# A hybrid decoder trunk on one core: another order of the first loads, and of the first gate weight ahead of the conformer

## The chip, the cores and the metric

The kernel runs on one core of a Trainium2 chip. The core has TensorE (PE), VectorE (DVE), ScalarE (ACT), GpSimd (POOL) and SyncE (SP), each with its own instruction stream, and 16 DMA engines that are fed from queues on SP, ACT and POOL. The metric is the time of one execution on the device, in microseconds (us), as the median of several runs.

## The reference, cut to what matters

Two layers work on 512 tokens of width 1024, all in float32. Layer 0 begins with a mixer, layer 1 with a conformer module; every layer goes on with cross-attention into 256 memory tokens and a gated MLP, each behind an RMSNorm and added to the residual.

```python
def rms_norm(x, g):
    y = xf * lax.rsqrt(jnp.mean(xf * xf, axis=-1, keepdims=True) + EPS)
    return (y * g).astype(x.dtype)

def conformer_conv(x, norm, w1, b1, dw_w, dw_b, ln_g, ln_b, w2, b2):
    h = rms_norm(x, norm) @ w1 + b1
    h = jax.nn.glu(h, axis=-1)
    h = causal_dwconv(h, dw_w, dw_b)
    h = jax.nn.silu(layer_norm(h, ln_g, ln_b))
    return h @ w2 + b2

def cross_attn(x, mem, norm, mem_norm, wq, wk, wv, wo):
    m = rms_norm(mem, mem_norm)
    k = (m @ wk).reshape(Bn, M, XA_HEADS, XA_HD)
    v = (m @ wv).reshape(Bn, M, XA_HEADS, XA_HD)
    ...
```

## The kernel before, in words

Activations lie feature by token: eight chunks X[0] to X[7] of 128 features by 512 tokens. Every matrix product is made of three: each operand is split into a high half (a copy rounded to the matmul's float type, on ACT: L170, L180, L204, L284) and a low half (the difference, on DVE: L171, L185, L207), and `mm3` (L190 to L192) adds high by high, high by low and low by high. So a weight of 128x1024 passes through DMA (tile `raw`, three buffers), ACT (`whi`) and DVE (`wlo`) before PE can use all of it, and its `raw` buffer comes free for a later load when DVE is done.

**Opening** (L1819 to L1924). The first work is the values of the cross-attention's memory, m @ wv: `mem.sums` (L458 to L469) takes one half of a weight a step, six products of 512 columns, L468. The gains `par` and the first half of the first weight are loaded from ACT's queue (L122, L123), all else from SP's in the written order: the memory's first half in pieces of 128x256 (L1836), the rest of the first weight, and so on, with the fourth weight behind the release of the first one's buffer. `mem.operand` splits a piece of the memory (ACT L399, DVE L400); `half` splits half a weight. Before that PE runs ten matmuls of 128x128 on a constant (L143), whose result nobody reads. In this stretch the order on PE, ACT, DVE, POOL and SP is the written one.

**Start of the conformer** (L1633 to L1673). The last weights of the MLP before it end in eight sums into X[n] (L911), each of which `Scaled.feed` (L254 to L259) follows with a square (ACT, L256) and an addition of the squares (DVE, L258). `norm.scale` then makes the factor of each token: column sums on PE (L324), a root (ACT, L331), a reciprocal (DVE, L332), two diagonal matrices (DVE, L337) and two products that spread them over the partitions (PE, L360). With it `norm.scaled`, `norm.high`, `norm.low` make each chunk of the normed input. As work for PE meanwhile there are keys of the second layer's memory (`mem.products` of parked weights: three pieces of 24 products of 256 columns), and then the first gate and value weights G0 and V0 multiply the normed chunks. Here Tile's scheduler sets the order of ACT and DVE by priority, except in the block of `norm.scaled/high/low`, which is written out, and from L1663 on, where all is written out again. `tc.issue_after(ins)` keeps an instruction behind `ins` on its engine.

Of the kernel before, what the change touches and what calls it, by code (L numbers as in the profile page):

```python
# [10 lines left out]
F32 = mybir.dt.float32  # L11
# [51 lines left out]
def trunk(ctx: ExitStack, tc: tile.TileContext, I: dict, out: list):  # L63
# [16 lines left out]
    def nm(s):  # L80
        uid[0] += 1
        return f"{s}_{uid[0]}"
# [7 lines left out]
    def big_f():  # L90
        return big.tile([P, 2 * T], F32, tag="big", name=nm("big"))
# [25 lines left out]
    G.memset(eps, EPS)  # L117
    A.activation(small.tile([P, 1], F32, tag="warm", name="warm", bufs=1), eps, AF.Copy)
    par = cpool.tile([P, NPAR], F32, tag="par", name="par")
    first_raw = wp.tile([P, D], F32, tag="raw", name="raw0", bufs=3)  # L120
    with tc.high_priority(AHEAD):
        A.dma_start(par[:, : 3 * C], I["params"][:, : 3 * C])  # L122
        A.dma_start(first_raw[:, :T], I["wv"][0][:, :T])  # L123
    xall = xpool.tile([P, C, T], F32, tag="x", name="x")
    X = [xall[:, c] for c in range(C)]

# [12 lines left out]
    V.tensor_copy(ones, onesf)  # L139

    idle = stat_ps()
    for _ in range(10):
        PE.matmul(idle[:, :P], onesf, onesf, start=True, stop=True)  # L143
    ident = cpool.tile([P, P], F32, tag="ident", name="ident")
    make_identity(nc, ident)
# [21 lines left out]
    def split(src, hi=None, lo=None, eng=None):  # L167
        hi = act_r() if hi is None else hi
        lo = act_r() if lo is None else lo
        A.activation(hi, src, AF.Copy)  # L170
        fetched[1] = (eng or V).tensor_tensor(lo, src, hi.bitcast(F32), op=ALU.subtract)  # L171
        return hi, lo
# [15 lines left out]
    def mm3(ps, w, x, first, last, onto=False):  # L188
        (wh, wl), (xh, xl) = w, x
        PE.matmul(ps, wh, xh, start=first, stop=False, skip_group_check=onto)  # L190
        PE.matmul(ps, wh, xl, start=False, stop=False, skip_group_check=onto)  # L191
        return PE.matmul(ps, wl, xh, start=False, stop=last, skip_group_check=onto)  # L192

    class Piece:


        def __init__(self, src, raw=None):
            self.raw = raw or wp.tile([P, D], F32, tag="raw", name=nm("raw"), bufs=3)
            fetched[0] = nc.sync.dma_start(self.raw, src)
# [9 lines left out]
    def blk(w, i, n=P):  # L209
        hi, lo = (w.hi, w.lo) if isinstance(w, Piece) else w  # L210
        if isinstance(hi, list):
            hi, lo, i = hi[i // T], lo[i // T], i % T
        return hi[:, i : i + n], lo[:, i : i + n]
# [33 lines left out]
    class Scaled:  # L247
# [6 lines left out]
        def feed(self, c):  # L254
            sq = tmp_f()
            self.square = A.activation(sq, X[c], AF.Square).ins  # L256
            if self.ss is not None:
                V.tensor_tensor(sq, self.ss, sq, op=ALU.add)  # L258
            self.ss = sq  # L259

        def scale(self):
# [65 lines left out]
    def token_scale(s, weight, halves):  # L327

        ps = token_sums(s, weight)
        rt = small.tile([P, 4], F32, tag="rtok", name=nm("rtok"), bufs=2)  # L330
        A.activation(rt, ps[:, :4], AF.Sqrt, bias=eps)  # L331
        V.reciprocal(rt, rt)  # L332
        return diagonals(rt, 4, halves)

    def diagonal(out, v, scale):
        n = v.shape[-1]
        V.scalar_tensor_tensor(  # L337
            out.rearrange("p (a b) -> p a b", a=n), ident.unsqueeze(1).broadcast_to([P, n, P]), scale,
            v.unsqueeze(2).broadcast_to([P, n, P]), op0=ALU.mult, op1=ALU.mult,
        )  # L340

    def diagonals(rt, n=4, halves=True):

# [37 lines left out]
    class Memory:  # L381
# [1 line left out]

        r = rt = None

        def __init__(self, layer, eng=None, load=True):
            self.layer, self.eng = layer, eng
            self.m = [big_f(), big_f()]
            self.xs = [None, None]
            if load:  # L390
                for h in range(2):
                    nc.sync.dma_start(self.m[h], I["mem"][h])
# [54 lines left out]
        def products(self, w, ps=None, ks=range(C)):  # L447
            ps = ps or mm_ps()
            for k in ks:
                mm3(ps[:, :M], blk(w, k * P), self.chunk(k), k == 0, k == C - 1)  # L450
            return ps

        def piece(self, i, **how):
# [1070 lines left out]
    def conformer(norm, nxt, mem, parked):  # L1524
# [88 lines left out]
        def warm(name, func, ins):  # L1613
            with tc.issue_after(ins):
                A.activation(small.tile([P, 1], F32, tag="warm", name=name, bufs=1), eps, func)
# [6 lines left out]
        def fetch():  # L1622
            if len(raws) < len(names):
                k, n = names[len(raws)][0], int(names[len(raws)][1:])
                src = I["pw1"][n + (C if k == "G" else 0)] if k in "GV" else I["wk" if k == "K" else "wv"][mem.layer * C + n]
                raws.append(wp.tile([P, D], F32, tag="raw", name=nm("raw"), bufs=3))
                Memory.fetched = nc.sync.dma_start(raws[-1], src)
# [2 lines left out]
            k = names[len(ws)]  # L1630
            ws[k] = load_w(raw=raws[len(ws)], eng=eng, park=k in ("R0", "R1", "R2", "R3"))

        for _ in range(2):  # L1633
            fetch()
            weights()
        for _ in range(3):
            fetch()
        warm("token", AF.Sqrt, norm.square)
        for n in range(KE):
            with tc.issue_after(mem.behind):  # L1640
                if n:
                    held = mem.products(parked[n])
                else:
                    mem.keys(n, parked[n])
            if n == 1:
                with tc.high_priority(URGENT):
                    norm.scale()
        with tc.high_priority(URGENT), tc.manual_schedule(engines={mybir.EngineType.Activation, mybir.EngineType.DVE}):
            norm.scaled(0)
            for c in range(C):  # L1650
                norm.high(c)
                if c + 1 < C:
                    norm.scaled(c + 1)
                norm.low(c)
                if c == 2:
                    split(held[:, :M], *mem.key(1))
            weights()
            fetch()
            weights()
# [157 lines left out]


    n0 = Scaled(("ab_norm", 0), False)  # L1819
    mem = Memory(0, load=False)  # L1820
    m = mem.m
    with tc.manual_schedule(engines=ORDERED | {mybir.EngineType.SP}):
        raws, ready = [first_raw], []

        def fetch(n, at=slice(0, D)):
            if n == len(raws):
# [3 lines left out]
        def half(n, i):  # L1830
            if n == len(ready):
                ready.append(tuple(wp.tile([P, D], F32R, tag=t, name=nm(t)) for t in ("whi", "wlo")))
            split(*[x[:, i * T : (i + 1) * T] for x in (raws[n], *ready[n])])

        for i in range(2):
            nc.sync.dma_start(m[0][:, i * M : (i + 1) * M], I["mem"][0][:, i * M : (i + 1) * M])  # L1836
        fetch(0, slice(T, D))
        nc.sync.dma_start(m[0][:, T:], I["mem"][0][:, T:])
        for i in range(2):
# [2 lines left out]
        fetch(2)  # L1842
        ps = [[mm_ps(), mm_ps()] for _ in range(2)]
        steps = mem.sums(0, ps[0], ready)
        for k in range(C):
            mem.operand(k // 4, [k % 4])
            half(k // 2, k % 2)
            next(steps)
            if k in (1, 3, 5, 7):
                fetch(k // 2 + 3)  # L1850
            if k == 3:
                nc.sync.dma_start(X[0], I["x"][0])
            elif k == 5:
                for c in (1, 2):
                    nc.sync.dma_start(X[c], I["x"][c])
# [155 lines left out]
```

## Time and profile before

| | us |
|---|---|
| median of 3 runs | 1419.03 (1418.37 to 1419.62) |
| the profiled execution | 1418.12 |
| its span in the trace | 1416.3 |
| PE busy in it | 1406.8 (99%) |
| DVE, ACT, POOL busy | 1142.8, 939.2, 317.8 |

The span is the time from the first to the last event that the profiler records; 1.8 us of the execution lie outside it. A timeline row gives the start, the duration, the engine, the line, the operation, output and input, and in brackets how long the engine had stood idle and what ended that.

### The profile page before, as it was taken

To read this page: it belongs to the slowest core of one execution; us is meant where nothing else is said; L and a number is where in the kernel's file an instruction comes from. 1 tells how busy PE (TensorE), PEld (TensorE's weight loads), DVE (VectorE), ACT (ScalarE), POOL (GpSimd) and SP (SyncE) were. 2 spreads that over 40 slices of the span, in tenths; PEclk is the share of its full clock that TensorE was granted. 3 is DMA by queue.
4 is the path that set the end of the run, shared out by engine and by line. 5 is a ranking of instruction groups with operands and counts; after the bars stand their busy time and mean duration, and the time that the engine had idled before them with its cause. 6 is when DMAs were issued, how large, how long until landed. Compare 5 with 4: busy or idle time off the path is not lost.

```text
span 1416.3 us, 21233 instructions
## 1 busy us (share of the span) xinstructions
PE 1406.8 (99%) x7700; PEld 1212.1 (86%) x7700; DVE 1142.8 (81%) x1932; ACT 939.2 (66%) x1692; POOL 317.8 (22%) x333
## 2 busy tenths in 40 slices
PE   9999999999999999999999999999999999999998
PEld 8888888998898888888888777899889888888887
DVE  6987776778877888888799997978788788788785
ACT  7678744776567676676666547766756766666664
POOL 0011310110122222222008993011002222212211
PEclk9999999999999999999999999999999999999999
DMA  8623232444387777677443454345438776776751
GB/s 309 194 75 103 91 119 82 111 121 128 99 204 173 164 180 178 162 180 170 122 119 119 120 157 156 105 90 131 111 101 194 174 179 164 174 182 163 169 136 60
DMA packets 80025, 204.22 MB, mean 144 GB/s; under 512 B 9008, under 2 KB 9520, under 8 KB 79920
## 3 DMA queue, kind: packets, MB, share of 16 engines
q1 hardware_dynamic: 50688, 149.89, 33.2%
q0 software_dynamic: 28800, 52.44, 21.6%
q8 instruction: 60, 0.98, 0.3%
q10 hardware_dynamic: 432, 0.54, 0.2%
q14 instruction: 45, 0.37, 0.1%
HBM read 145.16 MB, written 2.10 MB: 104 GB/s over the span
## 4 chain that ended last, share of the span: by engine, by line
PE 94%; DVE 3%; ACT 1%; DMA 1%; issue 1%; POOL 0%; ACTq 0%; POOLq 0%; DVEq 0%
PE mm L819 17%; PE mm L190 15%; PE mm L191 15%; PE mm L192 15%; PE aux L190 7%; PE aux L191 7%; PE aux L192 7%; PE stat L819 7%; PE mm L468 2%; PE mm L1569 1%; DVE wlo L171 1%; DVE act L171 1%; PE aux L542 0%; ACT whi L170 0%; PE aux L468 0%
## 5 line engine op out<-in xcount | busy, mean ns | idle before, releaser
L191 PE MATMUL mm<-act,whi 128*128 128x512 f32 (+2 forms) x779 | 288.1, 370 | 0.1
L190 PE MATMUL mm<-act,whi 128*128 128x512 f32 (+2 forms) x779 | 288.1, 371 | 0.0
L192 PE MATMUL mm<-act,wlo 128*128 128x512 f32 (+2 forms) x779 | 287.9, 370 | 0.0
L867 DVE TENSOR_TENSOR bigr<-raw,bigr 128x512 fp32r<-128x512 f32 x176 | 120.3, 686 | 62.7 <-ACT bigr L860 62.3
L190 PEld LDWEIGHTS mm<-act,whi 128*128 128x128 f32 x779 | 146.5, 188 | 25.7 <-ACT tmp L1594 0.8
L191 PEld LDWEIGHTS mm<-act,whi 128*128 128x128 f32 x779 | 146.8, 188 | 25.1 <-DVE act L171 1.0
L192 PEld LDWEIGHTS mm<-act,wlo 128*128 128x128 f32 x779 | 146.8, 188 | 24.7 <-DVE wlo L171 0.6
L860 ACT ACTIVATE bigr<-raw 128x512 fp32r<-128x512 f32 x176 | 109.3, 622 | 84.0 <-DVE wlo L207 81.5
L819 PE MATMUL mm<-bigr,bigr 128*128 128x512 f32 (+1 forms) x816 | 160.2, 338 | 0.0
L190 PE MATMUL aux<-act,whi 128*128 128x512 f32 x399 | 155.4, 390 | 0.0
L191 PE MATMUL aux<-act,whi 128*128 128x512 f32 x399 | 155.3, 389 | 0.0
L192 PE MATMUL aux<-act,wlo 128*128 128x512 f32 x399 | 155.2, 389 | 0.0
L873 POOL DMA_DIRECT2D raw<-wa x100 | 95.2, 972 | 254.0 <-DVE bigr L867 166.1
L170 ACT ACTIVATE whi<-raw 128x1024 fp32r<-128x1024 f32 (+1 forms) x95 | 96.2, 1019 | 83.9 <-PE mm L191 44.1
L819 PEld LDWEIGHTS mm<-bigr,bigr 128*128 128x128 f32 x816 | 120.9, 190 | 12.2
L870 POOL DMA_DIRECT2D raw<-raw x50 | 43.3, 866 | 385.6 <-DVE wlo L867 282.8
L171 DVE TENSOR_TENSOR wlo<-raw,whi 128x1024 fp32r<-128x1024 f32 (+1 forms) x75 | 90.3, 1210 | 19.9 <-ACT whi L170 19.6
L875 POOL DMA_DIRECT2D raw<-wa x50 | 43.1, 863 | 202.6 <-DVE bigr L867 91.1
L192 PEld LDWEIGHTS aux<-act,wlo 128*128 128x128 f32 x399 | 74.9, 188 | 15.8
L191 PEld LDWEIGHTS aux<-act,whi 128*128 128x128 f32 x399 | 74.9, 188 | 15.5
L190 PEld LDWEIGHTS aux<-act,whi 128*128 128x128 f32 x399 | 74.9, 188 | 15.4
L175 DVE TENSOR_TENSOR tmp<-mm,tmp 128x256 f32<-128x256 f32 x198 | 79.4, 418 | 3.4 <-PE mm L192 1.0
(384 smaller groups left out, 3336.1 us busy)
## 6 DMA issues: line engine op xcount, KB each, us to landing
raw<-wa POOLq DMA_DIRECT2D x150, 256.0 KB, 3.9
wa<-in_wpair SPq DMA_DIRECT2D x88, 256.0 KB, 3.7
raw<-in_wpair SPq DMA_DIRECT2D x44, 512.0 KB, 4.1
big<-in_wdown SPq DMA_DIRECT2D x42, 512.0 KB, 4.6
raw<-raw POOLq DMA_DIRECT2D x50, 256.0 KB, 4.0
raw<-in_pw SPq DMA_DIRECT2D x24, 512.0 KB, 3.9
raw<-in_win SPq DMA_DIRECT2D x20, 512.0 KB, 3.5
raw<-in_wk SPq DMA_DIRECT2D x16, 512.0 KB, 3.5
```

The source lines that it names most:

```text
L170: A.activation(hi, src, AF.Copy)
L171: fetched[1] = (eng or V).tensor_tensor(lo, src, hi.bitcast(F32), op=ALU.subtract)
L175: V.tensor_tensor(out, a, b, op=ALU.add)
L190: PE.matmul(ps, wh, xh, start=first, stop=False, skip_group_check=onto)
L191: PE.matmul(ps, wh, xl, start=False, stop=False, skip_group_check=onto)
L192: return PE.matmul(ps, wl, xh, start=False, stop=last, skip_group_check=onto)
L819: PE.matmul(to, part, x, start=first and i == 0, stop=i == 7, skip_group_check=True)
L860: A.activation(self.w[name][0], self.block(name), AF.Copy)
L867: V.tensor_tensor(lo, self.block(name), hi.bitcast(F32), op=ALU.subtract)
L870: G.dma_start(self.r, self.z, accum_op=ALU.add)
L873: G.dma_start(block, self.a22, accum_op=ALU.add)
L875: G.dma_start(self.r, self.a12, accum_op=ALU.add)
```

## The change

In the opening the two queues swap a load: ACT's queue now takes the first 128x256 piece of the memory (`first_mem`) behind the gains, and SP's begins with the first half of the first weight. The high half of that half weight is copied on DVE (`V.tensor_copy`) and not on ACT, ahead of DVE's first L400. The matmuls on a constant go from ten to eight.

At the start of the conformer the weight G0 is split only behind the last square and the last addition of squares (`norm.added`, `norm.square`), V0 behind the root and the second diagonal matrix (`token_scale.root`, `diagonal.last`). The column sums stand behind all 24 products of the first key (`keyed`). The first key's split moves into the written block, behind chunk 1, and the load of the fifth weight (G2) to chunk 3 of that block.

```diff
-    first_raw = wp.tile([P, D], F32, tag="raw", name="raw0", bufs=3)
+    first_mem = big_f()
     with tc.high_priority(AHEAD):
         A.dma_start(par[:, : 3 * C], I["params"][:, : 3 * C])
-        A.dma_start(first_raw[:, :T], I["wv"][0][:, :T])
+        A.dma_start(first_mem[:, :M], I["mem"][0][:, :M])
...
-    for _ in range(10):
+    for _ in range(8):
         PE.matmul(idle[:, :P], onesf, onesf, start=True, stop=True)
...
-        for _ in range(2):
-            fetch()
+        fetch()
+        with tc.issue_after(norm.added), tc.issue_after(norm.square):
             weights()
         for _ in range(3):
             fetch()
+        held = []
         warm("token", AF.Sqrt, norm.square)
         for n in range(KE):
             with tc.issue_after(mem.behind):
-                if n:
-                    held = mem.products(parked[n])
-                else:
-                    mem.keys(n, parked[n])
+                held.append(mem.products(parked[n]))
+            keyed = keyed if n else mem.last
             if n == 1:
-                with tc.high_priority(URGENT):
+                with tc.high_priority(URGENT), tc.issue_after(keyed):
                     norm.scale()
         with tc.high_priority(URGENT), tc.manual_schedule(engines={mybir.EngineType.Activation, mybir.EngineType.DVE}):
+            with tc.issue_after(token_scale.root), tc.issue_after(diagonal.last):
+                weights()
             norm.scaled(0)
             for c in range(C):
                 norm.high(c)
                 if c + 1 < C:
                     norm.scaled(c + 1)
                 norm.low(c)
-                if c == 2:
-                    split(held[:, :M], *mem.key(1))
+                if c in (1, 2):
+                    split(held[c - 1][:, :M], *mem.key(c - 1))
+                if c == 3:
+                    fetch()
             weights()
...
-            split(*[x[:, i * T : (i + 1) * T] for x in (raws[n], *ready[n])])
-
-        for i in range(2):
-            nc.sync.dma_start(m[0][:, i * M : (i + 1) * M], I["mem"][0][:, i * M : (i + 1) * M])
+            src, hi, lo = [x[:, i * T : (i + 1) * T] for x in (raws[n], *ready[n])]
+            if n or i:
+                split(src, hi, lo)
+            else:
+                low(src, hi, lo)
+
+        fetch(0, slice(0, T))
+        nc.sync.dma_start(m[0][:, M:T], I["mem"][0][:, M:T])
         fetch(0, slice(T, D))
...
+        ready.append(tuple(wp.tile([P, D], F32R, tag=t, name=nm(t)) for t in ("whi", "wlo")))
+        V.tensor_copy(ready[0][0][:, :T], raws[0][:, :T])
```

ACT's order at the very start, before (L123 loads the first half weight, L399 are pieces of the memory, L170 high halves of the weights `raw`):

```order
L122 DMA par<-in_params 128x24
L123 DMA raw_90<-in_wv 128x512
...
L399 ACTIVATE bigr_155<-big_137,par 128x256
L170 ACTIVATE whi_159<-raw_90 128x512
L399 ACTIVATE bigr_155<-big_137,par 128x256
L170 ACTIVATE whi_159<-raw_90 128x512
```

And after:

```order
L122 DMA par<-in_params 128x24
L123 DMA big_90<-in_mem 128x256
...
L399 ACTIVATE bigr_156<-big_90,par 128x256 x2
L170 ACTIVATE whi_153<-raw_138 128x512
L399 ACTIVATE bigr_156<-big_90,par 128x256
L170 ACTIVATE whi_181<-raw_143 128x512
```

One L170 has gone to DVE, and ACT's queue loads a piece of the memory.

DVE's order ahead of the conformer, before (the two L171 of 128x1024 are the low halves of G0 and V0, the one of 128x256 that of the first key, L911 the sum into the last chunk):

```order
L171 TENSOR_TENSOR wlo_7383<-raw_7380,whi_7382 128x1024
L258 TENSOR_TENSOR tmp_7358<-tmp_7341,tmp_7358 128x512
L911 TENSOR_TENSOR x<-x,mm_7361 128x512
L171 TENSOR_TENSOR wlo_7389<-raw_7386,whi_7388 128x1024
L258 TENSOR_TENSOR tmp_7375<-tmp_7358,tmp_7375 128x512
L332 RECIPROCAL rtok_7457<-rtok_7457 128x4
L351 CAST rhi_7460<-rtok_7457 128x4
L171 TENSOR_TENSOR bigr_7178<-mm_7400,bigr_7177 128x256
L337 SCALAR_TENSOR_TENSOR act_7462<-ident,rhi_7460 128x512
L353 TENSOR_TENSOR rlo_7461<-rtok_7457,rhi_7460 128x4
L337 SCALAR_TENSOR_TENSOR act_7463<-ident,rlo_7461 128x512
L278 SCALAR_TENSOR_TENSOR actf_7473<-x,par,aux_7468 128x512
```

And after:

```order
L258 TENSOR_TENSOR tmp_7356<-tmp_7339,tmp_7356 128x512
L911 TENSOR_TENSOR x<-x,mm_7359 128x512
L258 TENSOR_TENSOR tmp_7373<-tmp_7356,tmp_7373 128x512
L171 TENSOR_TENSOR wlo_7381<-raw_7378,whi_7380 128x1024
L332 RECIPROCAL rtok_7447<-rtok_7447 128x4
L351 CAST rhi_7450<-rtok_7447 128x4
L337 SCALAR_TENSOR_TENSOR act_7452<-ident,rhi_7450 128x512
L353 TENSOR_TENSOR rlo_7451<-rtok_7447,rhi_7450 128x4
L337 SCALAR_TENSOR_TENSOR act_7453<-ident,rlo_7451 128x512
L171 TENSOR_TENSOR wlo_7464<-raw_7384,whi_7463 128x1024
L278 SCALAR_TENSOR_TENSOR actf_7467<-x,par,aux_7458 128x512
```

G0's low half stands behind the last addition of squares, V0's between the second diagonal matrix and the first normed chunk, and the first key's has left this stretch.

PE's order at the column sums, before (mm_7400 is the first key, mm_7427 the second):

```order
L190 MATMUL mm_7400<-bigr_7167,act_7197 128x256
L191 MATMUL mm_7400<-bigr_7168,act_7197 128x256
L192 MATMUL mm_7400<-bigr_7167,act_7198 128x256
L190 MATMUL mm_7427<-bigr_7157,act_7209 128x256
L324 MATMUL stat_7452<-onesf,tmp_7375 128x1 x4
L191 MATMUL mm_7427<-bigr_7158,act_7209 128x256
```

And after (mm_7392 is the first key, mm_7417 the second):

```order
L190 MATMUL mm_7392<-bigr_7165,act_7195 128x256
L191 MATMUL mm_7392<-bigr_7166,act_7195 128x256
L192 MATMUL mm_7392<-bigr_7165,act_7196 128x256
L324 MATMUL stat_7442<-onesf,tmp_7373 128x1 x4
L190 MATMUL mm_7417<-bigr_7155,act_7207 128x256
L191 MATMUL mm_7417<-bigr_7156,act_7207 128x256
```

The column sums have moved up by one product; further on the two spreading products (L360) have moved down by four and by three, to behind the 19th and the 23rd product of the second key. No other engine or place changes its order, but for SP's: its list is one load longer at the start.

## Rows read from the trace of the kernel before

**Rows 1.** Timeline of the opening, all engines (columns: section on the profile).

```profile
0.74 0.86 SPq L1836 DMA_DIRECT2D big<-in_mem  x2
...
1.03 4.64 PE L143 MATMUL stat<-onesf 128*128 128x128 f32 x20 [1.03 <-POOL onesf L132]
...
1.18 0.46 ACTq L123 DMA_DIRECT2D raw<-in_wv  x1
...
5.30 0.63 ACT L170 ACTIVATE whi<-raw 128x512 fp32r<-128x512 f32 x1 [1.13 <-DMA raw<-in_wv]
...
5.99 0.50 PE L468 MATMUL mm<-whi,bigr 128*128 128x512 f32 x1 [0.32 <-ACT whi L170]
...
11.08 0.63 ACT L170 ACTIVATE whi<-raw 128x512 fp32r<-128x512 f32 x1 [0.77 <-DMA raw<-in_wv]
11.11 0.39 PE L468 MATMUL mm<-wlo,bigr 128*128 128x512 f32 x1
...
11.33 0.39 PE L468 MATMUL aux<-wlo,bigr 128*128 128x512 f32 x1
...
11.76 0.50 PE L468 MATMUL mm<-whi,bigr 128*128 128x512 f32 x1
```

**Rows 2.** DMA issues at 0.7 us: size of each, us to landing.

```profile
big<-in_mem SPq DMA_DIRECT2D x1, 128.0 KB, 2.7
```

**Rows 3.** DMA issues at 1.6 us, the same view.

```profile
raw<-in_wv ACTq DMA_DIRECT2D x1, 256.0 KB, 4.1
```

**Rows 4.** DMA issue at 4.2 to 4.6 us: the third weight.

```profile
raw<-in_wv SPq DMA_DIRECT2D x1, 512.0 KB, 7.0
```

**Rows 5.** Stretches: length, busy PE, PEld, DVE, ACT, POOL, granted clock, DMA share, GB/s.

```profile
3.00:4.00 1.00, 1.00 (x7) 1.00 (x7) 0.00 (x0) 0.89 (x4) 0.00 (x0) 1.00 0.51 157
4.00:5.00 1.00, 1.00 (x6) 1.00 (x6) 0.48 (x1) 0.17 (x1) 0.00 (x0) 1.00 1.04 373
1413.00:1416.30 3.30, 0.00 (x0) 0.00 (x0) 0.00 (x0) 0.00 (x0) 0.00 (x0) 0.50 0.40 147
```

**Rows 6.** Groups on DVE, first 30 us: busy us, mean ns, idle before.

```profile
L139 DVE CAST ones<-onesf 128x128 fp32r<-128x128 f32 x1 | 0.2, 226 | 1.0 <-POOL onesf L132 1.0
```

**Rows 7.** Timeline of PE at the start of the conformer.

```profile
724.73 0.39 PE L192 MATMUL mm<-act,wlo 128*128 128x512 f32 x1
...
727.83 0.28 PE L190 MATMUL mm<-bigr,act 128*128 128x256 f32 x1
728.68 1.05 PE L324 MATMUL stat<-onesf,tmp 128*128 128x1 f32 x8 [0.57 <-DVE tmp L258]
...
732.29 0.45 PE L360 MATMUL aux<-act,unit 128*128 128x512 f32 x1
...
734.36 0.40 PE L1668 MATMUL mm<-act,whi 128*128 128x512 f32 x1
```

**Rows 8.** Timeline of ACT there.

```profile
725.71 1.06 ACT L170 ACTIVATE whi<-raw 128x1024 fp32r<-128x1024 f32 x1 [1.25 <-DMA raw<-in_pw]
726.68 0.62 ACT L256 ACTIVATE tmp<-x 128x512 f32<-128x512 f32 x1
727.31 1.28 ACT L1615 ACT_TABLE_LOAD   x1
...
729.77 0.26 ACT L331 ACTIVATE rtok<-stat,eps 128x4 f32<-128x4 f32 x1 [0.97 <-PE stat L324]
...
733.55 1.29 ACT L284 ACTIVATE act<-actf 128x512 fp32r<-128x512 f32 x2 [3.24 <-DVE actf L278]
```

**Rows 9.** Timeline of DVE there.

```profile
725.72 0.68 DVE L911 TENSOR_TENSOR x<-x,mm 128x512 f32<-128x512 f32 x1
726.80 1.23 DVE L171 TENSOR_TENSOR wlo<-raw,whi 128x1024 fp32r<-128x1024 f32 x1 [0.41 <-ACT whi L170]
727.95 0.68 DVE L258 TENSOR_TENSOR tmp<-tmp,tmp 128x512 f32<-128x512 f32 x1
...
732.77 1.41 DVE L278 SCALAR_TENSOR_TENSOR actf<-x,par,aux 128x512 f32<-128x512 f32 x2 [0.60 <-PE aux L360]
```

More of the change, by code (lines that the diff above doesn't have):

```diff
@@ L257, in feed @@
             if self.ss is not None:
-                V.tensor_tensor(sq, self.ss, sq, op=ALU.add)
+                self.added = V.tensor_tensor(sq, self.ss, sq, op=ALU.add).ins
             self.ss = sq
@@ L330, in token_scale @@
         rt = small.tile([P, 4], F32, tag="rtok", name=nm("rtok"), bufs=2)
-        A.activation(rt, ps[:, :4], AF.Sqrt, bias=eps)
+        token_scale.root = A.activation(rt, ps[:, :4], AF.Sqrt, bias=eps).ins
         V.reciprocal(rt, rt)
@@ L336, in diagonal @@
         n = v.shape[-1]
-        V.scalar_tensor_tensor(
+        diagonal.last = V.scalar_tensor_tensor(
             out.rearrange("p (a b) -> p a b", a=n), ident.unsqueeze(1).broadcast_to([P, n, P]), scale,
             v.unsqueeze(2).broadcast_to([P, n, P]), op0=ALU.mult, op1=ALU.mult,
-        )
+        ).ins
     def diagonals(rt, n=4, halves=True):
@@ L384, in trunk, with __init__ @@
         r = rt = None
-        def __init__(self, layer, eng=None, load=True):
+        def __init__(self, layer, eng=None, load=True, first=None):
             self.layer, self.eng = layer, eng
-            self.m = [big_f(), big_f()]
+            self.m = [first or big_f(), big_f()]
             self.xs = [None, None]
@@ L449, in products @@
             for k in ks:
-                mm3(ps[:, :M], blk(w, k * P), self.chunk(k), k == 0, k == C - 1)
+                self.last = mm3(ps[:, :M], blk(w, k * P), self.chunk(k), k == 0, k == C - 1).ins
             return ps
@@ L1819, in trunk @@
     n0 = Scaled(("ab_norm", 0), False)
-    mem = Memory(0, load=False)
+    mem = Memory(0, load=False, first=first_mem)
     m = mem.m
     with tc.manual_schedule(engines=ORDERED | {mybir.EngineType.SP}):
-        raws, ready = [first_raw], []
+        raws, ready = [], []
         def fetch(n, at=slice(0, D)):
```

## The prediction

> **What bounds the kernel now.** I read the busy shares first, then PE's timeline for places where a product starts later than one product's length after the one before it, and there, on the engine named in the bracket, what came last. PE is busy for 1406.8 of 1416.3 us (table above), so an edit can give back only time in which PE stands or waits. In the two stretches that the change touches these are three. PE's first useful product starts at 5.99, when ACT has copied a half weight that landed at 5.3 [rows 1]. The steady distance of two 512-column products is 0.22 (11.11 to 11.33), but the next starts only at 11.76: 0.2 us lost, because the third weight landed at 11.08 [rows 1, 4]. And ahead of the conformer the column sums start at 728.68, while the product in front of them started at 727.83 and takes a step of 0.12 (24 such products make a key of 2.9 us): 0.73 us lost on the addition of the last square [rows 7]. Whatever the change wins elsewhere is beside PE's work.
>
> **The change part by part: the conformer.** Before, DVE added the last product sums at 725.72 to 726.4, ACT squared them from 726.68, behind the 1.06 us copy of V0, and DVE added the square from 727.95 to 728.63, behind V0's low half of 1.23 us [rows 8, 9]. After, both weights' splits stand behind this chain. PE's last product for the chunk starts at 724.73 and ends by 725.12 [rows 7]; add 0.68, square 0.62, add 0.68 with some 0.05 for each hand-over: the squares are ready at about 727.2. PE finishes the first key at 727.83, so the column sums go there without a wait, with 0.6 us in hand. PE's wait of 0.73 is gone.
>
> What is late next is the way from the sums to the first normed chunk, since G0 and V0 now stand in it.
> - Root: it came 1.09 us after the sums began (728.68 to 729.77), which gives 728.92. On ACT it also stands behind the last square (to 726.5), G0's copy 1.06 and the table load 1.28, that is 728.85 [rows 8]. I take 729.0; it is 0.77 earlier than before.
> - From root to second spreading product: 2.52 us before (729.77 to 732.29) [rows 7, 8]. The first key's low half (256 columns, an estimated 0.35 from the 0.68 of 512 columns) leaves this stretch, so the diagonals are ready at about 731.15. PE has its second spreading product behind 23 products of the second key: 727.83, sums 0.92 (an estimate from their 1.05, which overlaps what follows), 23 x 0.12, 0.24 for the first spreading product, gives 731.75. PE is the later.
> - First normed chunk: 0.48 after the spread before (732.29 to 732.77), so 732.25; but DVE has V0's low half in front, 731.15 + 1.23 = 732.4. Then 0.78 to ACT's copy and 0.65 to its end (732.77, 733.55, 734.2) [rows 8, 9]: ready at 733.7 to 733.85.
> - PE ends the second key at 732.15 and half of the third, 12 x 0.12, at 733.6, where it wants that chunk (L1668, 734.36 before) [rows 7]. So a wait of 0.1 to 0.25 takes the place of the 0.73.
>
> Gain 0.77 less 0.1 to 0.25; I take 0.6, bounds 0.45 and 0.77. The two key splits inside the written block cost DVE and ACT nothing on the path: DVE's loop takes about 1.3 us a chunk (0.68 twice, partly overlapped) and PE's 6 x 0.22 = 1.33, and only the first chunk is tight. V0's and G0's buffers come free about 4 us later, and with them the loads of V1 and G2 behind them on SP's queue; no other load that is wanted sooner is queued behind these two, and PE has 8 x 6 products of 0.22, 10.6 us, to do on G0 and V0 before it wants G1, and V1 and G2 only after that. Without that cover each would cost its lateness.
>
> **The opening.** SP's first issue, at 0.74, is now the 256 KB half weight, which on ACT's queue was issued at 1.18 and landed 4.1 later; the 128 KB piece goes the other way and took 2.7 from 0.74 [rows 1 to 3]. If each takes what it took before, the half weight lands at 4.8, the piece between 3.9 (by 2.7) and 5.3 (by 4.1). The DVE copy is not in the trace: 128 columns took 0.226 [rows 6], a 512-column subtraction 0.68 [rows 9], so it is bounded by 0.23 and 0.68; I take 0.4. The piece's split on ACT is another 0.5 (an estimate from 0.63 for 512 columns). PE's first product then starts between 4.8 and 5.9, likely at 5.3, against 5.99. The eight matmuls cost nothing: 0.8 x 4.64 from 1.03 ends at 4.74 [rows 1]. DVE's first L400 and low half now stand behind its copy, so the third pair of products may wait some 0.2; ACT is 0.63 freer.
>
> But four steps later PE wants the third weight, and already waits for it. The bytes ahead of it in the queues are the same and issued at the same moments; DMA moves 373 GB/s from 4 us on and is busy throughout, and only the stretch from 3 to 4 us is half empty (share 0.51, 157 GB/s) [rows 5]. If the earlier half weight filled that gap, (373 - 157) KB at 373 a us is 0.58, and with the 0.2 that PE already waits the third weight could no longer hold it: the gain would be the whole head start, 0.65 at most. If the gap is only moved, the gain is nought, since PE stands a longer time before 11.76. If the first loads now disturb each other, it may be a loss of 0.1. I take 0.1, nearest to the row at 11.76, bounds -0.1 and 0.65.
>
> The Trainium skill ("Trainium Kernel Development and Optimization", Key Constraints) speaks against this part: the queues of SP, ACT and POOL feed the same 16 engines and interleave, and issuing from several only saves issue time. By that rule the swap wins nothing in the third weight's landing, and the sum would be 0.6 and not 0.7. The trace agrees from 4 us on (share 1.04) and says nothing of the half-empty microsecond before.
>
> **Sum.** 0.6 + 0.1 = 0.7. Against the profiled execution: 1418.12 - 0.7 = 1417.4. That execution lies 0.9 below the median of the three runs, and the comparison will be of medians: 1419.03 - 0.7 = 1418.3.
>
> **Rivals.**
> - *The opening gives its whole head start.* The half-empty stretch from 3 to 4 us speaks for it, the wait at 11.08 on a full queue against it [rows 1, 5]. 0.6 + 0.65: 1417.8.
> - *The conformer's wait only moves to L1668.* If the last sum, square and addition are handed on more slowly than 0.05 each, or the root comes at its old distance from a later table load, V0's low half holds the first chunk: a root at 729.5 would give the chunk at 734.3, and the gain is nought to 0.2. It decides from a root later than about 729.1. The two long pieces that stand there now, 1.06 and 1.23, speak for it, the 0.6 us in hand at the sums against it. 1418.9.
> - *The change does not do what it says*: the piece on ACT's queue lands as late as the half weight did and the conformer's chain stays: 1419.0.
> - *Slower: the clock.* With eight matmuls PE stands idle from 4.74 until its first product, 0.1 to 1.1 us, against 0.32 before [rows 1]. The granted clock is 1.00 through the opening and 0.50 at the end, when PE has stood for some time [rows 5], that is 2.4 and 1.2 GHz. If it fell in the new gap and stayed down for the four steps, their 24 products would take 24 x 0.22 = 5.3 us more; starting at 5.3, PE would reach the fifth step at 15.9 and not 11.76, 4.1 later, and the sum is 1419.03 + 4.1 - 0.6 = 1422.5. It decides only when the low level holds for more than some three products, since 0.5 us before 11.76 are slack. The gap of 0.32 at a full clock speaks against it.
>
> The Trainium skill ("TensorE: Matmul & The Clock Gate", Part 1) states the rule behind this rival: the throttled state is the default, and activity releases it. The trace agrees in its last microseconds; no row shows whether so short a gap is enough.
>
> **How the numbers follow.** The forecast 0.53, the whole head start 0.22, the moved wait 0.16, nothing 0.05, the clock 0.04. A measurement of this kernel can tell about 0.2% from no change, which is 2.8 us. All cases but the clock lie within it: same 0.94, slower 0.04, faster 0.02, for a wait of PE that I haven't seen. The range takes in all but the clock and the faster one: from 1417.6 (0.77 + 0.65 less) to 1419.1 (a loss of 0.1), and half the spread of the three runs, 0.6, on each side, since the result is a median of few: 1417.0 to 1419.7.
>
> **What would show it.** Right: column sums directly behind the 24th product of the first key, with no wait on DVE; the root some 0.8 us nearer to the last MLP product; a wait of 0.1 to 0.25 before L1668. In the opening, the first product near 5.3 and a longer stand before the fifth step, with ACT's copy of the third weight still at about 11.1. Wrong: that copy at 10.6 or earlier (the head start is kept); a granted clock under 1.00 before 12 us; a wait at L1668 of 0.5 or more; or a new wait of PE after 60 us, which nothing in the order explains.

## The result: slower by about two microseconds

| | us |
|---|---|
| kernel before, median of 18 runs | 1418.46 (1416.73 to 1419.69) |
| changed kernel, median of 18 runs | 1420.5 (1419.25 to 1423.17) |
| ratio | 1.0016, 95% interval 1.001 to 1.0023 |
| the profiled execution of the changed kernel | 1423.17, span 1421.4 |

By the ratio the change costs 1.4 to 3.3 us. That is outside the range given. It is also less than the 0.2% that the prediction took for what can be told from no change, but with 18 runs of each kernel the interval leaves no change out. The profiled execution is the slowest of its 18, so its own 4.7 us are not the change's price. A second traced execution of this kernel, below, took 1422.39; none at the median was traced.

### The profile after: the opening

PE's timeline, and what releases it (columns as in [rows 1]):

```profile
1.03 3.78 PE L143 MATMUL stat<-onesf 128*128 128x128 f32 x16 [1.03 <-POOL onesf L132]
...
3.60 0.43 DVE L1853 CAST whi<-raw 128x512 fp32r<-128x512 f32 x1 [2.36 <-DMA raw<-in_wv]
5.04 0.91 ACT L399 ACTIVATE bigr<-big,par 128x256 fp32r<-128x256 f32 x2 [1.48 <-DMA big<-in_mem]
...
5.59 0.79 PE L468 MATMUL mm<-whi,bigr 128*128 128x512 f32 x1 [0.78 <-ACT bigr L399]
...
6.19 0.63 PE L468 MATMUL aux<-whi,bigr 128*128 128x512 f32 x1
6.61 0.63 PE L468 MATMUL mm<-whi,bigr 128*128 128x512 f32 x1
...
9.17 0.58 PE L468 MATMUL mm<-whi,bigr 128*128 128x512 f32 x1
...
9.60 0.39 PE L468 MATMUL aux<-whi,bigr 128*128 128x512 f32 x1
9.82 0.39 PE L468 MATMUL mm<-wlo,bigr 128*128 128x512 f32 x1
...
10.74 0.63 ACT L170 ACTIVATE whi<-raw 128x512 fp32r<-128x512 f32 x1 [0.77 <-DMA raw<-in_wv]
...
11.66 0.39 PE L468 MATMUL mm<-whi,bigr 128*128 128x512 f32 x1
```

The half weight lands at 3.6 and DVE copies it in 0.43, but the first product waits for the piece of the memory on ACT's queue, which lands at 5.0: 5.59 against 5.99 in [rows 1]. From there the distance from product to product is 0.43 (6.19 to 6.61), nine times with the first, of 0.60, and 0.22 only from 9.60 on; in [rows 1] it is 0.22 (11.11 to 11.33). The ratio is that of the clock's two levels, 1.2 and 2.4 GHz. Products at the longer distance are called slow below. The third weight is in time (its copy at 10.74), and PE does not wait for it; it is simply later.

The column that should tell this does not. Stretches of the changed kernel (columns as in [rows 5]):

```profile
4.80:5.60 0.80, 0.02 (x2) 0.01 (x1) 0.02 (x1) 0.56 (x2) 0.00 (x0) 1.00 0.99 302
5.60:9.60 4.00, 4.00 (x10) 3.13 (x11) 4.00 (x8) 3.05 (x7) 0.00 (x0) 1.00 1.00 375
9.60:12.00 2.40, 2.40 (x12) 1.98 (x11) 1.33 (x4) 1.63 (x4) 0.00 (x0) 1.00 0.97 340
```

The granted clock reads 1.00 over the slow products as over the quick ones, though 10 products fall in 4.0 us and then 12 in 2.4. The trace itself explains it. It keeps the clock as records of a start, a length and a level; the first one, at full, starts at 9.58 us, just where the steps shorten, and the view shows a stretch without any record as 1.00. That the level before it was the low one is read from the steps; near 1086, where the column does read 0.50, steps of 256 columns are 0.21 and not 0.12. The same column in [rows 5] was the prediction's evidence that the opening runs at full clock. In the trace of the kernel before the first record starts at 5.71, so those two stretches from 3 to 5 us hold none.

### The conformer

PE, ACT and DVE at the start of the conformer, in the order of time:

```profile
726.84 0.63 ACT L256 ACTIVATE tmp<-x 128x512 f32<-128x512 f32 x1 [2.15 <-DVE x L911]
727.38 1.04 ACT L170 ACTIVATE whi<-raw 128x1024 fp32r<-128x1024 f32 x1
727.51 0.69 DVE L258 TENSOR_TENSOR tmp<-tmp,tmp 128x512 f32<-128x512 f32 x1 [0.76 <-ACT tmp L256]
...
728.73 0.95 PE L324 MATMUL stat<-onesf,tmp 128*128 128x1 f32 x8
...
729.84 0.24 ACT L331 ACTIVATE rtok<-stat,eps 128x4 f32<-128x4 f32 x1
...
732.60 0.39 PE L360 MATMUL aux<-act,unit 128*128 128x512 f32 x1
733.08 1.40 DVE L278 SCALAR_TENSOR_TENSOR actf<-x,par,aux 128x512 f32<-128x512 f32 x2
733.86 1.29 ACT L284 ACTIVATE act<-actf 128x512 fp32r<-128x512 f32 x2 [2.82 <-DVE actf L278]
```

The column sums have no bracket: the wait of 0.57 in [rows 7] is gone. PE's last product of keys before the normed chunk and the first product with it:

```profile
734.26 0.28 PE L192 MATMUL mm<-bigr,act 128*128 128x256 f32 x1
734.54 0.50 PE L1671 MATMUL mm<-act,whi 128*128 128x512 f32 x1
```

A product of 256 columns takes a step of 0.12, so the 0.28 between these two starts holds a wait of 0.16. From the MLP's last product to the first with a normed chunk it is 8.91 us (725.63 to 734.54) against 9.63 in [rows 7]; over all twenty traced executions of this study it is 8.90 to 8.92 in the seven with the new conformer and 9.34 to 9.63, mean 9.44, in the thirteen with the old one. The gain is 0.53.

### A wait 350 us further on

Waits from 1076 to 1090 (engine, line, waited for: us, times, longest):

```profile
ACT bigr L860 <- DMA raw<-wa: 5.0, 1, 5.0
...
PE mm L190 <- ACT mm L997: 2.8, 1, 2.8
```

and the load behind them, issued by POOL at 1072.4 (KB, us to landing), then the same load in the kernel before:

```profile
raw<-wa POOLq DMA_DIRECT2D x1, 256.0 KB, 9.2
```

```profile
raw<-wa POOLq DMA_DIRECT2D x1, 256.0 KB, 5.2
```

This load adds to what its target holds. Issued at the same place, it lands 4 us later, ACT stands on it in its written order, and PE gets its bank late. PE's clock then falls as well:

```profile
1084.00:1086.00 2.00, 2.00 (x15) 2.00 (x14) 1.58 (x4) 0.68 (x1) 1.05 (x2) 0.69 0.76 143
1086.00:1088.00 2.00, 2.00 (x11) 2.00 (x11) 1.50 (x2) 0.60 (x3) 0.00 (x0) 0.50 0.90 155
```

Up to 1070 this execution is 0.35 behind the one of before; at 1090 it is 4.94 behind. The product that waits starts 3.0 late (the row above counts from the modelled end of the one before it), and 18 steps of 0.21 in place of 0.12 add 1.6; together they are these 4.6. No instruction there is touched by the change.

### The profile page after: what moved, and what is told of

The parts are those of the page before. It is cut to its first block, busy times and chain, and to the rows that moved or that the text cites. A ratio compares the mean times of both kernels' runs of the same rounds, so it can differ in the third digit from the quotient of the medians.

```text
span 1421.4 us, 21224 instructions
## 1 busy us (share of the span) xinstructions
PE 1409.1 (99%) x7696; PEld 1214.3 (85%) x7696; DVE 1143.7 (80%) x1933; ACT 938.8 (66%) x1691; POOL 317.5 (22%) x333
## 4 chain that ended last, share of the span: by engine, by line
PE 92%; issue 2%; DMA 2%; DVE 2%; ACT 1%; POOL 1%; ACTq 0%; SPq 0%; POOLq 0%; DVEq 0%
PE mm L819 17%; PE mm L190 14%; PE mm L191 14%; PE mm L192 14%; PE aux L190 7%; PE aux L191 7%; PE aux L192 7%; PE stat L819 7%; PE mm L468 2%; DMA raw<-wa 1%; PE mm L1569 1%; PE aux L542 0%; DVE wlo L171 0%; PE aux L468 0%; DMA big<-in_wdown 0%
## 5 line engine op out<-in xcount | busy, mean ns | idle before, releaser
L170 ACT ACTIVATE whi<-raw 128x1024 fp32r<-128x1024 f32 (+1 forms) x94 | 95.6, 1023 | 78.1 <-PE mm L191 43.1
L171 DVE TENSOR_TENSOR wlo<-raw,whi 128x1024 fp32r<-128x1024 f32 (+1 forms) x74 | 89.6, 1217 | 17.2 <-ACT whi L170 17.1
```

## The experiments

Theories at first: A, the eight matmuls leave TensorE at the low clock; B, the swapped loads or the copy on DVE cost; C, the conformer's new order or the wait near 1080. Each run is compared with runs of the kernel before on the same chip.

**Ten matmuls in the changed kernel, eight in the kernel before, and each half of the change alone.**

```diff
 # e1: the changed kernel
-    for _ in range(8):
+    for _ in range(10):
```

> The changed kernel with ten matmuls on a constant at the start and not eight. Theory A (TensorE's clock: with eight, PE stands idle from 4.8 us to the first useful product and goes on at 1.2 GHz until 9.6 us, as the product steps of 0.43 us in the changed kernel's trace show): with ten the steps are 0.23 from the first product, which starts near 5.7, and the time is 0.5 to 1.2 us below the kernel before (1417.3 to 1418.0 where it takes 1418.5). Theory B (the swapped loads or the copy on DVE cost the time): it stays about 2 us above the kernel before. Theory C (something in the conformer or behind it, as the 3 us wait at 1080 us in the changed kernel's trace): it stays 1 to 2 us above.

1419.23 (1417.28 to 1421.82, 11 runs) against 1419.2; ratio 1.0, interval 0.9991 to 1.0009. The first product starts at 5.86 and none is slow. The slowdown is gone, but level with the kernel before is not the 0.5 to 1.2 below it that A expected.

```diff
 # e2: the kernel before
-    for _ in range(10):
+    for _ in range(8):
```

> The kernel before with eight matmuls on a constant and nothing else changed. Theory A: PE stands idle from 4.8 us to 6.0 us, the product steps are 0.43 us for some microseconds, and it is 1.5 to 3 us slower than the kernel before. Theories B and C: no change, within 0.5 us, for the first product starts at 6.0 either way.

1421.79 (1419.41 to 1423.76); ratio 1.002, interval 1.0011 to 1.0029. PE:

```profile
1.03 3.78 PE L143 MATMUL stat<-onesf 128*128 128x128 f32 x16 [1.03 <-POOL onesf L132]
5.94 0.79 PE L468 MATMUL mm<-whi,bigr 128*128 128x512 f32 x1 [1.13 <-ACT whi L170]
6.53 0.63 PE L468 MATMUL aux<-whi,bigr 128*128 128x512 f32 x1
6.96 0.63 PE L468 MATMUL mm<-whi,bigr 128*128 128x512 f32 x1
...
9.52 0.55 PE L468 MATMUL mm<-whi,bigr 128*128 128x512 f32 x1
9.90 0.39 PE L468 MATMUL aux<-whi,bigr 128*128 128x512 f32 x1
```

One number changed in the kernel before gives a slowdown as large as the change's, and taking it out of the change removes it. On the cause of the slowdown A holds: the opening's other edits are not needed for it.

```diff
 # e3: the kernel before with the changed conformer;  e4: with the changed opening
```

> The kernel before with the conformer's part of the change alone. Theories A and B: 0.4 to 0.7 us faster than the kernel before, the wait of 0.73 us at the column sums gone, a wait of 0.1 to 0.3 ahead of the first product of the first gate weight in its place. Theory C: 1 to 2 us slower.

1418.93 (1417.4 to 1419.58); ratio 0.9996, interval 0.9987 to 1.0005.

> The kernel before with the opening's part of the change alone (loads, copy on DVE, eight matmuls). Theories A and B: 2.3 to 2.8 us slower than the kernel before, that is slower than the whole change by what the conformer's part gains. Theory C: within 0.5 us of the kernel before.

1421.47 (1419.85 to 1423.83); ratio 1.002, interval 1.0012 to 1.0029. In its one trace the clock had risen in time (steps 0.23 from 5.79), but the third weight came late:

```profile
11.86 0.63 ACT L170 ACTIVATE whi<-raw 128x512 fp32r<-128x512 f32 x1 [0.78 <-DMA raw<-in_wv]
```

against 11.08 in [rows 1]. So the opening holds the loss, and this trace shows a second piece in it beside the clock. Ten matmuls with the swapped loads bring no gain either (e1), though its conformer should have given 0.5 to 0.6.

**What it is about the matmuls: that PE stands behind them, or that they are few?**

```diff
 # e5 (and e9, e10): the kernel before; warmf is set by POOL behind its sixteen small sets
-        PE.matmul(idle[:, :P], onesf, onesf, start=True, stop=True)   # ten
+        PE.matmul(idle[:, :P], warmf, warmf, start=True, stop=True)   # eight
```

> The kernel before with eight matmuls on a constant and not ten, on a tile of their own that POOL sets behind its sixteen small sets; so they start some 0.9 us later than before and end where the ten ended, and PE stands before the first product no longer than it did with ten. POOL's set is the only other instruction added. Theory 'stand': eight matmuls cost 2.6 us (the run of the kernel before with eight) because PE stood 1.1 us before its first product. Then this kernel is level with the kernel before: -0.3 to +0.5, product steps 0.23 from the first or second product on. Theory 'amount': what counts is how much PE did before the products, with or without a stand. Then the steps are 0.43 for some eight products as with eight early ones: +2.0 to +3.0. I give the amount 0.6, the stand 0.4.

1420.14 (1418.91 to 1422.16); ratio 1.0015, interval 1.0006 to 1.0025. The eight run from 1.88 to 5.61, PE stands 0.18, and the steps of this trace are 0.23 from the first product. But the eleven times lie in two groups, six up to 1420.14 and five from 1421.3.

> The kernel with eight late matmuls, one more execution with its trace. Its eleven times lay in two groups, 1418.9 to 1420.1 and 1421.3 to 1422.2, and the one trace, of the first group, had steps of 0.23 from the first product on. Theory 'moment': in the second group the clock rises behind the first product, as with eight early ones, so an execution above 1421 shows some eight steps of 0.43, one below 1420.2 none or a few. Theory 'elsewhere': the groups come from a wait later on (near 1080 us, or at 1387), and steps are 0.23 from the start in both.

It took 1421.59, with slow steps:

```profile
6.32 0.79 PE L470 MATMUL mm<-whi,bigr 128*128 128x512 f32 x1 [0.66 <-ACT whi L172]
6.91 0.63 PE L470 MATMUL aux<-whi,bigr 128*128 128x512 f32 x1
7.33 0.63 PE L470 MATMUL mm<-whi,bigr 128*128 128x512 f32 x1
```

> The same kernel once more, for one more pair of time and trace; the same expectations as for the look before.

It took 1420.09, with three slow products, to 7.2. So the moment at which the clock rises differs from execution to execution of one program (the first clock record starts at 5.43, 10.12 and 7.16 in these three), and the two groups of times fit that. Closing the gap does not make eight safe: neither "stand" nor "amount" is the rule by itself.

```diff
 # e6: the kernel before
-    for _ in range(10):
-        PE.matmul(idle[:, :P], onesf, onesf, start=True, stop=True)
```

> The kernel before without any matmul on a constant (all ten are left out; their result is not used). Both theories expect product steps of 0.43 from the first product, 5.95, on. 'Stand': after a stand the eight matmuls were worth nothing, so the steps stay at 0.43 for some eight products as in the run with eight: +2.0 to +3.0, the same cost as with eight. 'Amount': the eight counted, and with none the slow steps last longer, by about what eight matmuls are in time, 3.7 us: some 17 products at 0.43 and not eight; they lose 17 x 0.21 = 3.6, of which the wait for the third weight, 0.2 to 0.5 us, takes some: +3.5 to +5.0.

1422.24 (1420.09 to 1423.67); ratio 1.0025, interval 1.0015 to 1.0035; fourteen slow products:

```profile
5.88 0.79 PE L465 MATMUL mm<-whi,bigr 128*128 128x512 f32 x1 [5.88 <-ACT whi L167]
...
11.17 0.63 PE L465 MATMUL mm<-whi,bigr 128*128 128x512 f32 x1
11.59 0.54 PE L465 MATMUL aux<-whi,bigr 128*128 128x512 f32 x1
11.97 0.40 PE L465 MATMUL mm<-whi,bigr 128*128 128x512 f32 x1
```

Leaving out all ten costs 3.6 us (1422.24 less 1418.67), leaving out two already 2.6 (e2).

> The changed kernel, one more execution with its trace. Its 18 times lie from 1419.25 to 1423.17, and the trace of the slowest one had nine steps of 0.43 and a wait of 2.8 near 1080 us. If the slow steps are what makes it slower than before in most executions, this trace has six to ten of them; if it has none, the time should be under 1420, unless the wait near 1080 us is there.

It took 1422.39, with eight slow products (5.77 to 9.25) and a wait of 2.1 near 1080.

> The kernel before with eight early matmuls, one more execution with its trace. By the theory that eight are too few, six to ten steps of 0.43 in most executions, and a fifth step that is not waited for; a time under 1420.3 only where the clock rose earlier, so with fewer slow steps, or where no wait is seen near 1080 us.

It took 1419.67, with no slow product and a wait of 2.0 near 1080. Here the clock rose in time (first record at 4.66), as expected for a low time.

**Is there a better kernel?**

```diff
 # e7: the kernel before with the changed conformer
-    for _ in range(10):
+    for _ in range(12):
```

> The changed kernel's conformer with the opening of before, and twelve matmuls on a constant and not ten. If in some executions of the kernel with ten the clock still rises behind the first product, two more should take these away: the median is 0 to 0.6 under that of the conformer alone with ten (run beside it), and the highest of its times falls. If the ten are enough, the two more cost their time where they end behind the landing of the first half weight: 1.03 + 12 x 0.43 = 6.2 at the latest against a first product at 5.9, 0 to +0.3 against the conformer alone. Against the kernel before: -1.2 to -0.2 by the first, -0.6 to -0.1 by the second.

1418.49 (1416.81 to 1419.81) against 1418.67; ratio 1.0002, interval 0.9993 to 1.001.

> The changed kernel's conformer with the opening of before and its ten matmuls, once more beside the others, for a second median and a second trace. The conformer's chain is worth 0.6 in all traces so far: -0.4 to -0.7 against the kernel before. If the conformer's gain were given back in the second half (a wait of PE near 1080 us behind a late load), it would be -0.2 to +0.5, and the trace would show that wait; if the wait near 1080 us is an event of single executions of any kernel, this trace may show it or not, and the median stays at -0.4 to -0.7.

1418.08 (1416.97 to 1419.05) against 1418.67; ratio 0.9997, interval 0.9988 to 1.0005. Twelve bring nothing measurable over ten. The conformer's 0.5 is plain in every trace and both medians lie below (0.3 and 0.6), but neither interval leaves out no change: no version here beats the kernel before measurably.

**The wait near 1080.** By then all traces with eight matmuls or none had it, and two of five with ten or twelve.

> The kernel before, one more execution with its trace. Theory 'any kernel': the wait of PE near 1080 us comes in most executions of every kernel, so in two of three of the kernel before, and the executions near 1419.5 have it while those near 1417.5 have not. Theory 'eight': it comes with eight matmuls only, all seven traces of such kernels have it; then an execution of the kernel before shows none, whatever its time. Both expect product steps of 0.23 from the first or second product.

It took 1418.05 and has no such wait.

> The kernel before again; the same expectations as for the look before this one.

It took 1419.61, with a wait of 1.4.

> The kernel before again; the same expectations as for the two looks before this one.

It took 1417.23, without the wait. So the kernel before has it too, in its slowest traced execution of four, and "eight only" falls.

> The changed kernel with ten matmuls once more. Theory 'any kernel': the wait near 1080 us in two of three executions, and a time near 1419.5 with it, near 1417.5 without it. Theory 'eight': the one trace of this kernel had the wait with ten matmuls, so this theory is already weak; without the wait here it is not dead, with it again it is. The third weight's copy on ACT between 10.7 and 11.3, steps of 0.23 from the first or second product.

It took 1420.04, with a wait of 1.6 and ten matmuls: "eight only" falls again. What goes with the wait is one row on SP's queue: in the execution of before, and in all so far that have no wait, the 512 KB load behind POOL's addition takes long to issue,

```profile
1072.03 0.86 POOL L873 DMA_DIRECT2D raw<-wa  x1 [2.04 <-DVE bigr L867]
1072.38 1.96 SPq L199 DMA_DIRECT2D big<-in_wdown  x1
```

and in those that have it (here the changed kernel) it does not:

```profile
1072.39 0.86 POOL L873 DMA_DIRECT2D raw<-wa  x1 [2.04 <-DVE bigr L867]
1072.78 0.42 SPq L199 DMA_DIRECT2D big<-in_wdown  x1
```

Long is 1.0 to 2.3 (five traces), short 0.38 to 0.45 in the thirteen with a wait. The two issues are 0.3 to 0.5 apart either way. Who gets served first may flip, but that is not shown, and the order of the rows doesn't tell why.

The wait did seem to go with a late start: all nine traces whose first column sums (L324, near 38 us) come at 38.4 or later had it, and four of nine earlier ones. A pure delay was tried on that.

```diff
 # e17: the kernel before;  e18: fifteen
-    for _ in range(10):
+    for _ in range(19):
```

> The kernel before with nineteen matmuls on a constant and not ten: a pure delay at full clock. Ten take 3.9 to 4.6 us, nine more at the step of the high clock 1.9, so the first product starts at 7.0 to 7.6 and not 5.9, and the opening's column sums at 38.7 to 39.2 and not 37.9: as late as with eight matmuls and nine slow steps. Theory 'late': the wait near 1080 us comes where the kernel arrives late, since all nine traces with column sums from 38.4 on have it and five of nine earlier ones have not. Then this kernel has it in its trace, and its median is +0.8 to +1.3 for the delay and +0.8 to +1.2 for the wait that now always comes: +1.7 to +2.5, with no time below 1418.9. Theory 'not late': the wait has its old frequency; +0.8 to +1.3, and some times near 1418.2.

1422.04 (1421.09 to 1423.5) against 1417.78; ratio 1.0025, interval 1.0016 to 1.0034: 2.3 to 4.8 us. Its column sums come at 39.65, 1.8 later, and no slow product. The wait near 1080 is *not* in its trace (the issue took 0.63); instead PE loses 0.3 to 0.7 at each of four places, near 60, 261, 386 and 712:

```profile
711.99 0.73 PE L190 MATMUL mm<-act,whi 128*128 128x512 f32 x2 [0.58 <-ACT act L984]
```

By this one trace "late brings the wait near 1080" falls. What holds is less: 1.8 us lost in the opening end as more than 1.8. In the trace all of it is lost ahead of the conformer, where the MLP's last product starts at 728.74, 4.1 behind the mean of the four traces of the kernel before.

> The kernel before with fifteen matmuls and not ten: five more take 1.1 us at the high clock, of which the wait ahead of the first product (0.2 to 0.9) and the wait for the third weight (0.2 to 0.6) take most, so the column sums come 0 to 0.4 later, at 37.9 to 38.3. Theory 'late': 0 to +0.8, since only some executions pass the point beyond which all have the wait near 1080 us. Theory 'not late': 0 to +0.4.

1419.33 (1417.4 to 1420.23); ratio 1.0006, interval 0.9998 to 1.0015; column sums at 37.94, a small wait of 0.6 near 1080. It tells nothing apart.

### The traces side by side

| kernel (traces) | slow products | first clock record, us | first column sums, us | wait near 1080, us |
|---|---|---|---|---|
| before (4) | 0, 0, 1, 0 | 5.71, 4.65, 6.28, 4.12 | 38.07, 38.32, 37.52, 37.53 | 0, 0, 1.4, 0 |
| conformer alone (2) | 0, 0 | 4.81, 5.82 | 37.93, 37.78 | 0, 1.5 |
| conformer, twelve | 0 | 4.20 | 37.84 | 0 |
| changed, ten (2) | 0, 0 | 6.03, 3.95 | 38.43, 38.76 | 1.8, 1.6 |
| opening alone | 0 | 5.38 | 38.56 | 1.8 |
| changed (2) | 9, 8 | 9.58, 9.11 | 38.91, 38.95 | 3.0, 2.1 |
| before, eight (2) | 9, 0 | 9.84, 4.66 | 39.19, 37.72 | 1.5, 2.0 |
| before, eight late (3) | 0, 9, 3 | 5.43, 10.12, 7.16 | 38.20, 39.57, 38.41 | 1.7, 2.0, 1.5 |
| before, none | 14 | 11.90 | 40.17 | 2.7 |
| before, nineteen; fifteen | 0; 0 | 7.20; 5.48 | 39.65; 37.94 | 0; 0.6 |

The slow products follow the first clock record in every row. The waits are counted from start to start of the two products, less a step.

Prices come out of the column sums. With the old loads and ten matmuls (at most one slow product) the mean of six is 37.86. The three traces with the swapped loads and no slow products lie at 38.58: there the swap *loses* 0.7. Their third weight's copy on ACT starts at 11.3, 11.5 and 11.9 against 10.4 to 11.2 in those six. In the two traces of the changed kernel, though, it starts at 10.74 and 10.97, within the old range, so the swap doesn't always make it late. Nine slow products cost 1.3 (39.19, one trace) with the old loads. With the swapped ones eight or nine end at 38.93, no later: PE doesn't stand for the third weight there, and the swap's loss is not seen in the changed kernel's own traces. The swapped loads and the copy on DVE were not tried apart.

## Why the prediction was wrong

**The step that failed: "the eight matmuls cost nothing".** Their time was right (0.8 of the ten's, ending at 4.81 where 4.74 was worked out), their task was not seen. The rival "the clock" named the mechanism and was given 0.04, because it asked whether the clock would *fall* in the gap, and because [rows 5] shows 1.00 at 3 to 5 us. The runs show that it starts low and has to *rise*. In the kernel before, the first clock record starts at 5.71 and the ten matmuls of [rows 1] end at 5.67: they ran at the low level, and it rose in the very gap of 0.32 that was held against the rival. e17 has the rise within the matmuls on a constant, its first record at 7.20. In stretches of one microsecond:

```profile
6.00:7.00 1.00, 1.00 (x7) 1.00 (x7) 1.00 (x3) 0.93 (x3) 0.00 (x0) 1.00 1.11 322
7.00:8.00 1.00, 1.00 (x10) 1.00 (x10) 0.83 (x2) 0.84 (x3) 0.00 (x0) 1.00 0.98 354
```

7 records of the same matmul before, 10 behind (a record that overlaps the edge of a stretch counts in both), and the clock column says 1.00 in both. The rival's size was too large (24 slow products, 4.1 us); it was eight or nine in four of the eight traces with eight matmuls, three in one and none in three. The Trainium skill ("TensorE: Matmul & The Clock Gate", Part 1) has the throttled state as the default that activity releases; the traces agree, with fourteen products at 0.43 where nothing ran before them, and the prediction cited the sentence and then followed the column against it.

**The opening's swap: +0.1 forecast, bounds -0.1 to 0.65, measured -0.7 where the clock rose in time (38.58 in three traces less 37.86 in six).** The head start came, smaller than worked out: the first product at 5.5 to 5.9 (5.3 forecast) against 5.8 to 6.0 with the old loads and ten matmuls, since the piece on ACT's queue took 3.8 and not 2.7. But the bounds kept the third weight's landing at about 11.08 or earlier, since "the bytes ahead of it in the queues are the same", with 0.1 for loads that disturb each other. In those three traces it landed some 0.7 later than in the six; in the changed kernel's own two it did not. Why the same bytes in another order can take longer was not tried. The Trainium skill's rule that all queues share 16 engines ("Trainium Kernel Development and Optimization", Key Constraints) was on the right side in saying that the swap wins nothing here; the loss in the three traces went past it.

**The conformer: right, with its steps, in the profiled execution.** Squares ready at 728.2 (727.2 forecast, and this execution starts 0.9 later); column sums without a wait; the root 4.21 us behind the MLP's last product and not 5.04, 0.83 nearer (0.8 forecast); a wait of 0.16 in its place (0.1 to 0.25); 0.53 gained, from the means of the traces (0.6). No interval of times shows it.

**What was not in the sum.** The forecast took everything behind 60 us as unchanged, and named a new wait there as a sign of being wrong; it came. The opening's loss is 1.07 in the two traces of the changed kernel (38.93 less 37.86), the conformer gives 0.53 back, and that leaves +0.5 of a measured +1.4 to +3.3. The rest lies behind 1070 in both: in the wait that the kernel before shows in one of four traces and the changed kernel in both of its own, and in the clock that fell after it in both traces of the latter. In no other of the twenty did it fall there, not even behind e6's wait of 2.7. An estimate for an execution without that fall: 0.5 and a wait of 1.6 to 2.1, as in the four other traces with the swapped loads, make 2.1 to 2.6, and the medians differ by 2.0. That the waits are more frequent is the reading of few traces; why a wait comes in one execution and not in the next, and whether the opening brings it, stays open. e17 says nothing on it: its delay grew from 1.8 to 4.1 ahead of the conformer, and 2.3 to 4.8 was the cost in its times.

## What to carry over

Matmuls on a constant ahead of the first load are there for the clock, and their number is to be judged by the distance between products of equal size behind them, in several traces, not by their own time. Where a column for the clock reads full at the start of a trace, compare product steps there with those in mid-kernel before trusting it: here it meant that nothing was recorded yet. In this kernel a head start on the first load was worth nothing, since PE waits for a later one anyway, and another order of the loads could cost what that later one needs.

## What the hardware showed that was not expected

- The clock starts low, and the traces don't record it: the first record of the clock, at full, starts between 3.95 and 11.90 us, and the steps ahead of it are 0.43 where they are 0.22 behind (5.6 to 9.6 in the changed kernel), under a column that reads 1.00.
- One program raises its clock at different moments: with eight matmuls from 1.88 on, at 5.43, 7.16 and 10.12 in three executions. With nineteen, which ran without a break from 1.03, it was 7.20, later than the first product of the kernel before; so ten, with 3.95 to 6.28 in eight traces, need not always be enough.
- An adding load issued by POOL next to a 512 KB load on SP's queue lands in 3.9 to 6.1 us in the six traces without the wait near 1080, in 6.7 in e18 with its wait of 0.6, and in 7.6 to 9.2 us in the thirteen with a wait of 1.4 or more. The four traced executions of the kernel before part by it: 1417.23 to 1418.12 without the late landing, 1419.61 with it.
